# Decode keys in plain fp32, prepared two steps ahead, with part sums by matmul, in a hybrid encoder layer

## The chip, the cores and the metric

The kernel runs as one program on one core of a Trainium2 chip. Its time is the device time of one execution in microseconds. A profile of one execution is read beside it. The engines are PE (TensorE; PEld is its weight load), DVE (VectorE), ACT (ScalarE), POOL (GpSimd) and SP (SyncE, which here only issues DMAs).

## What is computed

One layer of a streaming encoder, for a prompt of 1024 tokens and for 8 decode sequences of 16 new tokens each, 9 tiles of 128 tokens in all; the model width is 1024. Cut to what matters:

```
def trunk_layer(x, p, ...):
    h = rmsnorm(x, g_mix)
    q_a, k_a, v_a, q_b, k_b, v_b = split_heads(h, w_in)     # 2 groups of 8 heads x 64
    # group A, all the past:  z = q k / 8
    #   w = exp(log_sigmoid(z) + reverse cumulative sum of log_sigmoid(-z));  a = w v
    # group B, own chunk of 64 and the 8 before it:
    #   o_b = softmax(q k / 8 + rel_table[clipped distance]) v
    # decode: the keys and values of the past come from caches
    #   (A: 1024 rows, B: 512 rows a sequence), then the 16 new ones
    mix = concat(rmsnorm per head(a), rmsnorm per head(o_b))
    x = x + mix @ w_out
    h = rmsnorm(x, g_ffn)
    x = x + (silu(h @ w_gate) * (h @ w_up)) @ w_down        # d_ff 2816
    x = x + sigmoid(rmsnorm(x, g_ple) @ w_ple_gate) * (p @ w_ple_proj)
    return rmsnorm(x, g_final), new keys and values
```

## The kernel before, in words

**Precision.** Most products are made of fp32 numbers split in two float32r parts, a high one and a low one (the remainder). `mm3` (L104 to L107) multiplies them as three matmuls: high by high, high by low, low by high. A split is a cast on ACT and a subtraction (`sub`, L109) on DVE or POOL; `Chunks` (L124 on) does it for weights and cache rows: `raw` issues the DMA (L134), `pair` gives the two tiles, `parts` casts on ACT (L149) and subtracts on POOL.

**Order.** The program is written with Python generators. `project`, `dec`, `att` and the smaller ones yield after each step, and `advance(main, side, ratio)` interleaves two of them. The framework then plans each engine's queue in simulated time, with program order as priority; a later instruction can go ahead of an earlier one that waits, if its tiles have room. On the chip each engine's queue runs in that planned order. Tiles come from pools of SBUF or PSUM banks; a new pool may lie where a closed one lay, and its tiles then wait for the old ones there.

**Stages.**
1. `x` is loaded, normed and transposed in nine tiles (`transposed`, L182; `normed`, L192).
2. `qkv` projects to queries, keys and values in twelve loads of 256 columns. `loads` begins with A's queries. A query step (`queries`) uses weights as the stationary operand and three token tiles (384 columns) as the moving one; a step of keys or values (`others`) uses one token tile. Keys are turned on PE (L255). High and low parts go to DRAM (`qkT`, `vhl`). 36 steps run alone, 30 more beside decode A (2.2 decode steps to one), the rest beside attention (1.95 attention steps to one).
3. `decode(grp, ...)`, for group A (4 chunks of 256 cache rows a sequence) and later B (2 chunks): a step of kind "k" turns 256 keys on PE (L385), casts them to high parts on ACT (L387) and subtracts low parts on DVE, then makes scores by `mm3` against a block-diagonal query (`scores`); a step of kind "v" splits values on ACT and POOL, flips the weights (`flip`) and accumulates (`outputs`, L457, L458). Each step's inputs are prepared one step ahead; `finish` picks the diagonal, sums parts with the constant `sel` (L474), norms, and writes to DRAM.
4. `attention` treats the prompt in 8 pairs of heads, A's four and then B's four, each with 2 heads of 8 query tiles: units. Per unit: `scores` (L564, L565, then sigmoids and a scan for A, a reduction with bias and an exp for B); five units later `flip` (L598, cast L602, subtraction); one later `outputs` (L621, L622). The product gives two halves on 128 partitions (from the high and the low parts of v); ACT copies one half (L628) and DVE adds (L629). After a pair, `finish` turns it (L640), norms it (L642 to L660) and writes it to DRAM (`mixp`, L663).
5. Beside attention B run decode B, then `embed` (the projection of p, L782 to L794), then `half_out`: `mix` reads `mixp` and `mixs` back, turns it (L829) and splits it; then the upper half of the output projection is added to `x1` in SBUF (L849).
6. After attention: mix of pairs 4 to 7, the lower half of the output projection with norm and transposes (`lower`), the feed-forward, the gated embedding, the final norm.

**PSUM, eight banks.** Up to the end of decode A: left t=2, o=2, s=1 (the stack `first`), right d=2, a=1 (`dstack`). For attention: left s=2, t=3, and right o=3 for the rest of the projection, opened after both earlier stacks close. Then right d=2, a=1 for decode B, and m=2 for the mix.

Of the kernel before, what the change touches and what calls it, by code (L numbers as in the profile page):

```python
# [22 lines left out]
P = 128  # L23
# [11 lines left out]
VLAG = (2, 1)  # L35
# [3 lines left out]
def tile_hymba_step(  # L39
# [55 lines left out]
    V.memset(zero, 0.0)  # L95

# [107 lines left out]
    mixp = [dram.tile([NP * P, P], F32, name=f"mixp{i}") for i in range(8)]  # L204
    proj = dram.tile([NT * P, D], F32, name="proj")
    mixs = [dram.tile([8 * P, HD], F32, name=f"mixs{i}") for i in range(2)]
# [5 lines left out]
    def qkv(ch, hT, stg):  # L212

        def parts(n, src, scale=1.0):
            hl = [stg.tile([P, 384], F32R, name=f"st{x}", tag=f"st{x}", bufs=1 + (x == "h"))[:, :n] for x in "hl"]
# [12 lines left out]
        def queries(grp, c, wts):  # L228
            wh, wl = wts
            for pr in range(2):  # L230
                m = slice(pr * P, (pr + 1) * P)
                for g in range(3):
# [3 lines left out]
                    transposed_out(grp, 0, c * 2 + pr, g, parts(384, ps_, HD**-0.5))  # L236
                    yield

        def others(grp, w, c, wts, gs):

            wh, wl = wts
            for g in gs:
# [14 lines left out]
                else:  # L257
                    for o in range(3):
                        sv = stg.tile([P, 4, 2, HD], F32R, name="sv", tag="sv", bufs=2)
# [21 lines left out]
        loads = [(0, 0, 0), (0, 0, 1), (0, 1, 0), (0, 1, 1), (0, 2, 0), (0, 2, 1),  # L281
# [26 lines left out]
    def decode(grp, ch, dk):  # L308
# [12 lines left out]
        new = {}  # L321
        for what in "qk":
            for x in range(2):
                t_ = dk.tile([P, 4, P], F32R, name=f"s{what}{x}")
                nc.sync.dma_start(t_.bitcast(F32), qkT[grp]["qk".index(what)][x][:, :, NP * P :].rearrange("c p n -> p c n"))
                new.setdefault(what, []).append(t_)
# [3 lines left out]
        new["v"] = [sv[:, :, :, x, :] for x in range(2)]  # L330
        qbd = []
        for i in range(2):
            pair = [dk.tile([P, 4, P], F32R, name=f"qbd{i}{j}") for j in range(2)]
            for t_ in pair:
                G.tensor_copy(t_, zero.unsqueeze(1).broadcast_to([P, 4, P]))
            qbd.append(pair)
        yield
# [14 lines left out]
        def prepare(i):  # L352
# [10 lines left out]
            if c == 0:  # L363
                q = st["q"] = qbd[n % 2]
                for part in range(2):
                    for half in range(2):
                        s = slice(half * 64, half * 64 + 64)

                        flat = q[part].rearrange("p a b -> p (a b)")[s]
                        dst = bass.AP(  # L370
                            tensor=flat.tensor,
                            offset=flat[:, half * 16 : half * 16 + 1].offset,
                            ap=[flat.ap[0], [160, 4], [1, 16]],
                        )
                        G.tensor_copy(dst, new["q"][part][s, :, b * 16 : b * 16 + 16].bitcast(F32))
# [4 lines left out]
            nk = 272 if last else 256  # L380
            kh, kl = ch.pair(4, nk)
            for m in range(2):
                pt = ps["d"].tile([P, 512], F32, name="pt", tag="T")
                for pr in range(4):
                    T.transpose(pt[:, pr * P : (pr + 1) * P], raw[:, m, pr * P : (pr + 1) * P], ident)  # L385
                pv = pt.rearrange("p (k n) -> p k n", k=4)
                A.copy(kh[:, :, m * P : (m + 1) * P], pv)  # L387
                sub(V, kl[:, :, m * P : (m + 1) * P], pv, kh[:, :, m * P : (m + 1) * P])
            if last:
                for dst, src in zip((kh, kl), new["k"]):  # L390
                    G.tensor_copy(dst[:, :, 256:272], src[:, :, b * 16 : b * 16 + 16].bitcast(F32))
            split[i] = kh, kl, None
# [13 lines left out]
        def scores(st, c, kh, kl):  # L406
# [5 lines left out]
            for pr in range(4):  # L412
                mm3(sc, q[0][:, pr], q[1][:, pr], kh[:, pr], kl[:, pr], pr == 0, pr == 3 and (grp == 1 or not last))
# [5 lines left out]
            else:  # L419
                mx = dk.tile([P, 1], F32, name="mx", tag="mx", bufs=4)  # L420
                V.tensor_tensor_reduce(w, sc, bias[:, own], 1.0,
                                       -3e38 if st["mx"] is None else st["mx"], ALU.add, ALU.max, accum_out=mx)
                st["mx"] = mx

        def weights(st):
# [8 lines left out]
            else:  # L434
# [3 lines left out]
                V.tensor_scalar(mx, mx, -1.0, None, op0=ALU.mult)  # L438
                A.activation(w, w, AF.Exp, bias=mx, accum_out=sm)
# [8 lines left out]
        def outputs(st, c, vh, vl, wt):  # L448
# [11 lines left out]
            if c == 0:  # L460
                add(wt[:, 0], *new["v"], True, False)
# [3 lines left out]
        def finish(st):  # L465
            b, acc = st["b"], st["acc"]
            own = dk.tile([P, 2, 64], F32, name="own", tag="own", bufs=2)
            av = acc.rearrange("p q (h d) -> p q h d", h=4)
            for h in range(4):
                s = slice(h * 32, h * 32 + 32)  # L470
                (V.tensor_copy if h % 2 else A.copy)(own[s], av[s, :, h, :])
            po = ps["d"].tile([P, 64], F32, name="po", tag="T")
# [12 lines left out]
            nc.sync.dma_start(mixs[grp][b * P : (b + 1) * P, :], ow)  # L485

        for i in range(RAWS - 1):
            fetch(i)
        prepare(0)
        for i, (kind, n, c) in enumerate(seq):  # L490
            if i + RAWS - 1 < len(seq):
                fetch(i + RAWS - 1)
            if i + 1 < len(seq):
                prepare(i + 1)
            h, l, wt = split.pop(i)
            if kind == "k":
                scores(batch[n], c, h, l)
                if c == nkc - 1:
                    weights(batch[n])
            else:  # L500
                outputs(batch[n], c, h, l, wt)
                if c == nkc - 1:
                    finish(batch[n])
            yield


    def attention(qp, ap_, ps, lag):
        def prepare(p8):
            grp, pr = divmod(p8, 4)
            st = {"pr": pr, "grp": grp}  # L510
            if grp:
                st["rs"] = ap_.tile([P, NP, 2], F32, name="rsum", tag="rsum", bufs=2)
            return st

        def head(st, hh):
# [4 lines left out]
            hd = {}  # L520
            qk = ap_.tile([P, 2 * D], F32R, name="qk", tag="qk", bufs=2)
            vk = ap_.tile([P, 2 * D], F32R, name="vk", tag="vk", bufs=2)
            for dst, parts in ((qk[:, :D], (qh, ql)), (qk[:, D:], (kh, kh)), (vk[:, D:], (kl, kl))):
                for i in range(2):
                    nc.sync.dma_start(dst[i * 64 : i * 64 + 64].bitcast(F32), parts[i][hs, :D])
            hd["qq"], hd["kkh"], hd["kkl"] = qk[:, :D], qk[:, D:], vk[:, D:]
            vv = vk[:, :D].rearrange("p (t x d) -> p t x d", t=NP, x=2)
            hc = ((pr % 2) * 2 + hh) * P
            nc.sync.dma_start(
                vk[:, :D].bitcast(F32).rearrange("p (t n) -> p t n", t=NP),  # L530
                vhl[grp][pr // 2, : NP * P, hc : hc + P].rearrange("(t p) n -> p t n", p=P),
            )
            hd["v"] = vv
            st[hh] = hd
# [3 lines left out]

        def bias(st, hh):
            toep = ap_.tile([P, (8 - hh * 2) * P], F32, name="toep", tag=f"keep{1 + hh}")[:, :640]  # L540
            nc.sync.dma_start(toep, rel[st["pr"] * 2 + hh])
            G.memset(toep[0:64, 576:640], NEG)
            G.memset(toep[64:128, 0:64], NEG)
            st[hh]["toep"] = toep

        def scores(st, hh, t):
# [11 lines left out]
            for lo, hi in ((0, cut), (cut, n)):  # L558
# [12 lines left out]
                else:  # L571
                    m = ap_.tile([P, 1], F32, name="mxp", tag="mxp", bufs=6)
                    V.tensor_tensor_reduce(w[:, lo:hi], sc, hd["toep"][:, 640 - n + lo : 640 - n + hi], 1.0,
                                           -3e38 if mx is None else mx, ALU.add, ALU.max, accum_out=m)
# [5 lines left out]
            else:  # L580
                V.tensor_scalar(mx, mx, -1.0, None, op0=ALU.mult)
                A.activation(w, w, AF.Exp, bias=mx, accum_out=st["rs"][:, t, hh : hh + 1])
# [23 lines left out]
        def outputs(st, hh, g, wt):  # L606
# [4 lines left out]
            po = ps["t"].tile([P, 512], F32, name="pt", tag="T")  # L611
            order = [2 * g] + [kb for kb in range(base, 2 * g + 2) if kb != 2 * g]
            for i, kb in enumerate(order):
# [8 lines left out]
                T.matmul(dst, lhsT=vs, rhs=wtl[:, kb - base, c0:c1], start=False, stop=(i == nkb - 1))  # L622

            if hh == 0 and g == 0:
                st["ob"] = ap_.tile([P, D], F32, name="ob", tag="ob", bufs=1)
# [419 lines left out]
```

## Time and profile before

| | us |
|---|---|
| median of 3 runs | 1995.54 |
| lowest, highest | 1991.24, 1997.32 |
| profiled execution, its own time | 1995.02 |
| its span, first to last instruction | 1993.2 |
| PE busy in the span | 1859.9 |
| mean granted TensorE clock | 0.971 |

Line numbers (L105) are those of the kernel before. An engine's busy time is the union of its records; PE's records overlap, since a matmul starts before the one ahead of it has ended. So a PE that is shown busy may still have room, and the distance between two starts says more. In a list of stages each row has the window, its length, and for each engine the busy time and the number of records; then the granted clock, the busy share of the DMA engines and their GB/s. In a list of groups the last two parts are busy time with the mean of one in ns, and the idle time just before, with what ended it. In a list of waits the figures are total time, times, longest.

### The profile page before, as it was taken

To read this page: it belongs to the slowest core of one execution; us is meant where nothing else is said; L and a number is where in the kernel's file an instruction comes from. 1 tells how busy PE (TensorE), PEld (TensorE's weight loads), DVE (VectorE), ACT (ScalarE), POOL (GpSimd) and SP (SyncE) were. 2 spreads that over 40 slices of the span, in tenths; PEclk is the share of its full clock that TensorE was granted. 3 is DMA by queue.
4 is the path that set the end of the run, shared out by engine and by line. 5 is a ranking of instruction groups with operands and counts; after the bars stand their busy time and mean duration, and the time that the engine had idled before them with its cause. 6 is when DMAs were issued, how large, how long until landed. Compare 5 with 4: busy or idle time off the path is not lost.

```text
span 1993.2 us, 29599 instructions
## 1 busy us (share of the span) xinstructions
PE 1859.9 (93%) x11682; PEld 1737.9 (87%) x11682; DVE 828.1 (42%) x1573; ACT 740.4 (37%) x1595; POOL 716.5 (36%) x602
## 2 busy tenths in 40 slices
PE   5999999789997888879699999999999999999998
PEld 4999998679996777668589999999999999999898
DVE  5112445537767566464352213213213213213635
ACT  5214555547666667563333111111111111111442
POOL 4113744547645454022123232232232232232355
PEclk8999999899998899989799999999999999999999
DMA  5546766545547486592211111111111111111133
GB/s 188 184 167 195 225 221 206 171 129 140 160 131 220 135 205 161 168 267 60 85 49 64 43 43 43 43 43 43 43 43 43 43 43 43 43 43 43 33 96 127
DMA packets 164682, 220.70 MB, mean 111 GB/s; under 512 B 14912, under 2 KB 116160, under 8 KB 164544
## 3 DMA queue, kind: packets, MB, share of 16 engines
q1 hardware_dynamic: 164544, 218.82, 36.5%
q8 instruction: 92, 1.51, 0.3%
q14 instruction: 46, 0.38, 0.1%
HBM read 168.97 MB, written 49.81 MB: 110 GB/s over the span
## 4 chain that ended last, share of the span: by engine, by line
PE 53%; DMA 4%; issue 3%; ACT 1%; POOL 1%; DVE 1%; SPq 0%; POOLq 0%; ACTq 0%
PE ps L105 16%; PE ps L106 15%; PE ps L107 15%; DMA proj<-pjo 1%; PE acc L105 1%; PE acc L106 1%; PE acc L107 1%; DMA mixn<-mixp 1%; PE pt L188 1%; DMA qk<-qT1l 1%; DMA vk<-kT1l 0%; PE pt L598 0%; POOL dlo L110 0%; PE pt L829 0%; DMA vk<-v 0%
## 5 line engine op out<-in xcount | busy, mean ns | idle before, releaser
L110 POOL TENSOR_TENSOR wlo<-wraw,whi 128x1024 fp32r<-128x1024 f32 (+1 forms) x112 | 263.1, 2369 | 606.6 <-ACT whi L149 597.1
L105 PE MATMUL ps<-hUh,whi 128*128 128x384 f32 x1056 | 352.9, 334 | 2.2 <-DVE sg L912 2.2
L106 PE MATMUL ps<-hUl,whi 128*128 128x384 f32 x1056 | 353.0, 334 | 0.0
L107 PE MATMUL ps<-hUh,wlo 128*128 128x384 f32 x1056 | 352.9, 334 | 0.0
L149 ACT CAST whi<-wraw 128x1024 fp32r<-128x1024 f32 (+1 forms) x112 | 108.5, 1018 | 319.7 <-PE ps L107 227.4
L928 DVE TENSOR_TENSOR x<-x,ps 128x512 f32<-128x512 f32 x198 | 136.0, 687 | 158.1 <-PE ps L107 158.1
L105 PEld LDWEIGHTS ps<-hUh,whi 128*128 128x128 f32 x1056 | 198.2, 188 | 3.0 <-DVE sg L912 2.6
L106 PEld LDWEIGHTS ps<-hUl,whi 128*128 128x128 f32 x1056 | 198.2, 188 | 0.4
L107 PEld LDWEIGHTS ps<-hUh,wlo 128*128 128x128 f32 x1056 | 198.2, 188 | 0.0
L107 PE MATMUL ps<-whi,hTl 128*128 128x256 f32 x576 | 165.7, 288 | 0.0
L105 PE MATMUL ps<-whi,hTh 128*128 128x256 f32 x576 | 165.4, 287 | 0.1
L106 PE MATMUL ps<-wlo,hTh 128*128 128x256 f32 x576 | 164.7, 286 | 0.0
L106 PE MATMUL ps<-wlo,acth 128*128 128x512 f32 x396 | 156.2, 394 | 0.0
L105 PE MATMUL ps<-whi,acth 128*128 128x512 f32 x396 | 155.3, 392 | 0.0
L107 PE MATMUL ps<-whi,actl 128*128 128x512 f32 x396 | 153.8, 388 | 0.0
L110 POOL TENSOR_TENSOR dlo<-draw,dhi 128x1024 fp32r<-128x1024 f32 x48 | 117.2, 2445 | 101.6 <-ACT dhi L149 99.1
L914 DVE TENSOR_TENSOR tmp<-sg,ps 128x384 f32<-128x384 f32 x66 | 36.6, 554 | 235.4 <-PE ps L107 235.4
L912 DVE TENSOR_TENSOR sg<-tmp,ps 128x384 f32<-128x384 f32 x66 | 36.5, 554 | 196.5 <-ACT tmp L911 196.4
L110 POOL TENSOR_TENSOR actl<-tmp,acth 128x384 fp32r<-128x384 f32 x66 | 66.6, 1010 | 133.7 <-ACT acth L915 133.7
L578 DVE TENSOR_TENSOR_SCAN keep<-keep,zero 128x128 f32<-128x128 f32 (+4 forms) x64 | 97.5, 1528 | 37.1 <-ACT keep L570 36.6
L105 PEld LDWEIGHTS ps<-whi,hTh 128*128 128x128 f32 x576 | 109.7, 190 | 0.5 <-DVE stl L221 0.3
L106 PEld LDWEIGHTS ps<-wlo,hTh 128*128 128x128 f32 x576 | 109.7, 190 | 0.2
(188 smaller groups left out, 4400.4 us busy)
## 6 DMA issues: line engine op xcount, KB each, us to landing
draw<-in_cache_sb_k SPq DMA_DIRECT2D x32, 512.0 KB, 4.7
draw<-in_cache_sb_v SPq DMA_DIRECT2D x32, 512.0 KB, 3.9
wraw<-in_w_in SPq DMA_DIRECT2D x12, 1024.0 KB, 6.2
wraw<-in_w_gate SPq DMA_DIRECT2D x11, 1024.0 KB, 5.4
wraw<-in_w_up SPq DMA_DIRECT2D x11, 1024.0 KB, 5.4
wraw<-in_w_down SPq DMA_DIRECT2D x11, 1024.0 KB, 5.0
v<-sv SPq DMA_DIRECT2D x36, 256.0 KB, 2.4
x<-in_x_prompt SPq DMA_DIRECT2D x16, 512.0 KB, 6.8
```

What stands on the lines that cost most here:

```text
L105: T.matmul(out, lhsT=ah, rhs=bh, start=start, stop=False)
L106: T.matmul(out, lhsT=ah, rhs=bl, start=False, stop=False)
L107: T.matmul(out, lhsT=al, rhs=bh, start=False, stop=stop)
L110: eng.tensor_tensor(out, a, hi.bitcast(F32), op=ALU.subtract)
L149: A.copy(h[:, o], v[:, o])
L188: T.transpose(pt[:, j * P : (j + 1) * P], h[:, c : c + P], ident)
L578: V.tensor_tensor_scan(rev, rev, zero[:, 0:1].to_broadcast([P, n]), 1.0, op0=ALU.mult, op1=ALU.add)
L912: V.tensor_tensor(out[0][:, f, s], t_, ps, op=ALU.mult)
L914: V.tensor_tensor(t_, sg[:, f, s], ps, op=ALU.mult)
L928: V.tensor_tensor(x1[t][:, o], x1[t][:, o], ps, op=ALU.add)
```

## The change

What it does, part by part:
- **Keys of decode** stay in fp32 after their turn: one tile `kT` (3 buffers) in place of a high and a low one, half copied by ACT, half by DVE; the query is the sum of its two parts; one fp32 matmul replaces `mm3`. Key turns use bank pool t in place of d. Inputs are prepared `AHEAD` = 2 steps ahead, the diagonal is copied at once and the rest of `finish` comes two steps later. B's cache rows have 3 buffers in place of 4.
- **Banks.** o=2 is opened once, on the right, for the whole projection; attention has t=4 in place of 3; decode B has d=1.
- **Order of loads.** A's keys come before its queries.
- **Sign.** B's queries, bias and rel tables are negated, and the softmax takes a minimum and `scale=-1`, so that the maximum needs no negation (L435, L581).
- **Part sums.** `outputs` of attention only copies both halves (ACT, 128x256); `turn`, per head, sums and turns them with a fp32 matmul against `halves` (two stacked identities). `outputs` comes two units after `flip`.
- **Heads.** `values` loads v apart from `head`; both are issued at the unit t=1 instead of 3, B's first head at t=6 of pair 3.
- **Embedding** runs along decode B (one step to 0.55), its tiles turned one ahead, `pjo` with 2 buffers.
- **Mix.** `mix` fetches two pieces ahead, and takes pairs as they finish; pair 7 is taken from SBUF; `mixs` is written in its final layout.
- **Residual.** The upper half's sum goes to DRAM (`resid`) and is read to `x1` after attention's SBUF is free.

The core of the diff:

```diff
-VLAG = (2, 1)
+VLAG, AHEAD = (2, 1), 2
...
+    halves = cst.tile([P, HD], F32, name="halves")
+    V.tensor_tensor(halves, ident[:, :HD], ident[:, HD:], op=ALU.add)
...
-        loads = [(0, 0, 0), (0, 0, 1), (0, 1, 0), (0, 1, 1), (0, 2, 0), (0, 2, 1),
+        loads = [(0, 1, 0), (0, 1, 1), (0, 0, 0), (0, 0, 1), (0, 2, 0), (0, 2, 1),
...
-            kh, kl = ch.pair(4, nk)
+            kT = dk.tile([P, 4, 272], F32, name="kT", tag="kT", bufs=AHEAD + 1)
             for m in range(2):
-                pt = ps["d"].tile([P, 512], F32, name="pt", tag="T")
+                pt = ps["t"].tile([P, 512], F32, name="pt", tag="T")
...
-                A.copy(kh[:, :, m * P : (m + 1) * P], pv)
-                sub(V, kl[:, :, m * P : (m + 1) * P], pv, kh[:, :, m * P : (m + 1) * P])
+                (A.copy, V.tensor_copy)[m](kT[:, :, m * P : (m + 1) * P], pt.rearrange("p (k n) -> p k n", k=4))
...
-                mm3(sc, q[0][:, pr], q[1][:, pr], kh[:, pr], kl[:, pr], pr == 0, pr == 3 and (grp == 1 or not last))
+                T.matmul(sc, lhsT=q[:, pr], rhs=kT[:, pr, :nk], start=(pr == 0),
+                         stop=(pr == 3 and (grp == 1 or not last)))
...
-            if i + 1 < len(seq):
-                prepare(i + 1)
+            if i + AHEAD < len(seq):
+                prepare(i + AHEAD)
...
-            own, other = slice(hh * 64, hh * 64 + 64), slice(64 - hh * 64, 128 - hh * 64)
-            tmp = ap_.tile([P, 256], F32, name="obt", tag="obt", bufs=1)
-            A.copy(tmp[own], po[other, :256])
-            V.tensor_tensor(st["ob"][own, g * 256 : g * 256 + 256], po[own, :256], tmp[own], op=ALU.add)
+            A.copy(st["ob"][:, g * 256 : g * 256 + 256], po[:, :256])
+
+        def turn(st, hh):
...
+            pt = ps["t"].tile([P, 512], F32, name="pt", tag="T")
+            for t in range(NP):
+                T.matmul(pt[:, t * HD : (t + 1) * HD], lhsT=st["ob"][:, t * P : (t + 1) * P], rhs=halves,
+                         start=True, stop=True)
+            own = st["osb"][:, :, hh * HD : (hh + 1) * HD]
+            A.copy(own, pt.rearrange("p (t d) -> p t d", t=NP))
...
-    banks(first, "left", t=2, o=2, s=1)
+    banks(right, "right", o=2)
+    banks(first, "left", t=2, s=1)
...
-    banks(left, "left", s=2, t=3)
-    banks(right, "right", o=3)
+    banks(left, "left", s=2, t=4)
...
-    banks(dstack, "right", d=2, a=1)
+    banks(dstack, "right", d=1, a=1)
...
-    beside = chain(dec, embed())
-    advance(att, beside, 1.3, 42)
+    next(dec)
+    advance(att, dec, 0, 6)
+    beside = along(dec, embed(), 0.55)
+    advance(att, beside, 1.3, 40)
...
+        if k < 7:
+            nc.sync.dma_start(src, mixp[k][g * 384 : g * 384 + n * P, :].rearrange("(t p) c -> p t c", p=P))
+        else:
+            src = pairs[7]["osb"][:, g * 3 : g * 3 + n]
...
+                nc.sync.dma_start(resid[t * P : (t + 1) * P, cs], xs)
...
-    side = half_out()
+    side = chain(half_out(), mix(range(4, 7)))
     advance(att, side, 1.0)
+    for _ in side:
+        pass
+    for _ in mix([7]):
+        pass
+    w_b = [out_weights(1, c) for c in range(2)]
     left.close()
...
+    for t in range(NT):
+        nc.sync.dma_start(x1[t], resid[t * P : (t + 1) * P, :])
```

More of the change, by code (lines that the diff above doesn't have):

```diff
@@ L329, in decode @@
                           vhl[grp][:, NP * P :, :].rearrange("c p n -> p c n"))
[L330 to L337, printed above, removed]
+        new_v = [sv[:, :, :, x, :] for x in range(2)]
+        qbd = [dk.tile([P, 4, P], F32, name=f"qbd{i}") for i in range(2)]
+        for t_ in qbd:
+            G.memset(t_, 0.0)
         batch = [{"b": b} for b in range(8)]
@@ L364, in prepare @@
                 q = st["q"] = qbd[n % 2]
[L365 to L375, printed above, removed]
+                for half in range(2):
+                    s = slice(half * 64, half * 64 + 64)
+                    flat = q.rearrange("p a b -> p (a b)")[s]
+                    dst = bass.AP(
+                        tensor=flat.tensor,
+                        offset=flat[:, half * 16 : half * 16 + 1].offset,
+                        ap=[flat.ap[0], [160, 4], [1, 16]],
+                    )
+                    G.tensor_copy(dst, new_q[s, :, b * 16 : b * 16 + 16])
                 st["w"] = dk.tile([P, nkc * 256 + 16], F32, name="wdec", tag="w", bufs=3)
@@ L502, in decode, with attention @@
                 if c == nkc - 1:
-                    finish(batch[n])
+                    diagonal(batch[n])
+                    late[i + AHEAD] = batch[n]
+            if i in late:
+                finish(late.pop(i))
             yield
-    def attention(qp, ap_, ps, lag):
+        for st in late.values():
+            finish(st)
+    def attention(ap_, ps, lag):
         def prepare(p8):
@@ L668, in run @@
             ws, wts = {}, {}
-            for i in range(len(units) + lag + 2 + 2):
+            for i in range(len(units) + lag + 4):
                 if i < len(units):
                     pr, hh, t = units[i]
-                    if t == 3:
+                    if t == 1:
+                        values(st[pr], hh)
                         if hh == 0:
@@ L776, in embed, with turned @@
         wj = ch.load(w_ple_proj[0].rearrange("(k p) c -> p k c", p=P), 2, D)
-        for t in range(NT):
+        def turned(t):
             pn = pp.tile([P, 256], F32, name="pn", tag="pn")
@@ L799, in chain, with along @@
             yield from p_
-    beside = chain(dec, embed())
-    advance(att, beside, 1.3, 42)
+    def along(a, b, ratio):
+        due = 0.0
+        for _ in a:
+            yield
+            due += ratio
+            while due >= 1.0:
+                due -= 1.0
+                if next(b, "end") != "end":
+                    yield
+        yield from b
+    next(dec)
+    advance(att, dec, 0, 6)
+    beside = along(dec, embed(), 0.55)
+    advance(att, beside, 1.3, 40)
     for _ in beside:
@@ new lines, in turn_mix, with mix @@
+    def turn_mix(k, g, srcs):
+        pt = ps["m"].tile([P, 384], F32, name="pt", tag="M")
+        for o, src in enumerate(srcs):
+            T.transpose(pt[:, o * P : (o + 1) * P], src, ident)
+        h, l = hT.rows(g, k)
+        gk = g_out[:, k : k + 1]
+        A.activation(h, pt, AF.Copy, scale=gk)
+        V.scalar_tensor_tensor(l, pt, gk, h.bitcast(F32), op0=ALU.mult, op1=ALU.subtract)
+    def mix(ks):
+        got = []
+        for k in ks:
+            while k not in done:
+                yield
+            for g in range(3):
+                got.append((k, g, fetch_mix(k, g)))
+                if len(got) > 2:
+                    turn_mix(*got.pop(0))
+                yield
+        for x in got:
+            turn_mix(*x)
@@ L834, in mix @@
             yield
     def half_out():
-        for k in range(4):
-            yield from mix(k)
+        yield from mix(range(4))
         for c in range(2):
```

227 lines of the change are left out of this document (111 added, 116 removed).

## The prediction

> **What bounds the kernel now.** I read the page first (busy shares, slices), then the busy time by stage, the same for the projection's tile alone, then single timelines, groups and waits where a term needed a price.
>
> ```profile
> span 1993.2 us, 29599 instructions
> PE 1859.9 (93%) x11682; PEld 1737.9 (87%) x11682; DVE 828.1 (42%) x1573; ACT 740.4 (37%) x1595; POOL 716.5 (36%) x602
> PE   5999999789997888879699999999999999999998
> PEclk8999999899998899989799999999999999999999
> ```
>
> The profiled execution took 1995.02 us around its span of 1993.2, so 1.8 us lie outside; the median of the runs is 1995.54. I make the sum against 1995. The last 23 slices are full: that is the feed-forward, which the change does not touch. The time to be had lies in the first slice and between slices 7 and 20. By stage:
>
> ```profile
> core 0: us, PE busy (x) PEld busy (x) DVE busy (x) ACT busy (x) POOL busy (x), PEclk, DMA share, GB/s
> 17.80:56.00 38.20, 28.55 (x142) 26.36 (x143) 19.21 (x26) 14.02 (x25) 13.75 (x16) 0.82 0.45 155
> 160.00:325.00 165.00, 165.00 (x1407) 164.68 (x1406) 70.69 (x104) 82.65 (x182) 78.36 (x81) 1.00 0.67 211
> 325.00:415.00 90.00, 65.47 (x428) 58.40 (x427) 44.22 (x65) 42.91 (x92) 51.07 (x38) 0.85 0.49 158
> 415.00:600.00 185.00, 182.65 (x1337) 172.67 (x1336) 123.98 (x162) 119.47 (x293) 107.38 (x82) 1.00 0.56 153
> 600.00:770.00 170.00, 137.73 (x965) 125.01 (x965) 115.55 (x297) 118.17 (x270) 89.81 (x113) 0.91 0.68 186
> 770.00:850.00 80.00, 67.04 (x400) 55.80 (x399) 42.52 (x140) 47.23 (x118) 12.39 (x15) 0.98 0.57 158
> 850.00:900.00 50.00, 38.96 (x236) 33.55 (x235) 33.10 (x118) 34.15 (x84) 10.44 (x10) 0.86 1.01 269
> 900.00:960.00 60.00, 59.76 (x318) 50.86 (x317) 28.93 (x80) 17.61 (x42) 9.93 (x6) 1.00 0.17 41
> 960.00:998.00 38.00, 20.39 (x107) 16.14 (x105) 12.15 (x26) 13.45 (x26) 9.88 (x6) 0.73 0.41 120
> ```
>
> These are: the start of the projection; decode A beside the projection; the end of decode A; attention on group A beside the projection's rest; attention beside decode B; beside the embedding; beside the mix transposes; beside the half output projection; the tail. What a PE matmul really occupies is the distance between two starts, which is shorter than its record:
>
> ```profile
> start us, us, engine line op out<-in xcount [idle before <-releaser]
> 229.06 0.28 PE L106 MATMUL ps<-wlo,hTh 128*128 128x256 f32 x1
> 229.18 0.28 PE L107 MATMUL ps<-whi,hTl 128*128 128x256 f32 x1
> 229.54 0.56 PE L474 MATMUL po<-own,sel 128*128 128x64 f32 x4
> 229.93 0.28 PE L397 MATMUL pt<-ident,wn 128*128 128x128 f32 x1
> ...
> 1200.17 0.33 PE L106 MATMUL ps<-hUl,whi 128*128 128x384 f32 x1
> 1200.34 0.34 PE L107 MATMUL ps<-hUh,wlo 128*128 128x384 f32 x1
> 1200.51 0.39 PE L105 MATMUL ps<-whi,acth 128*128 128x512 f32 x1
> 1200.74 0.39 PE L106 MATMUL ps<-wlo,acth 128*128 128x512 f32 x1
> ```
>
> A split matmul over 256 columns takes 0.12 us of PE, one over 384 takes 0.17, one over 512 takes 0.23. At 0.12 each, the 428 matmuls of 325 to 415 are 51 us of work: 39 us are empty, more than the busy column admits. From 600 to 770, 965 x 0.12 = 116, 54 empty. From 770 to 850, 108 of the 400 are the embedding's (18 outputs of 6 matmuls) at 0.23: 25 + 292 x 0.12 = 60, 20 empty. From 850 to 900, 236 x 0.12 = 28, 22 empty. From 960 to 998 some 13 to 16 of 38, 22 empty. So 325 to 998 holds about 157 empty us; 160 to 325 and 900 to 960 hold none. From 600 to 900 no engine is full (DVE 0.64, ACT 0.67): that stretch is bound by waits between engines.
>
> The hole at 325 has one reason:
>
> ```profile
> 160.00:325.00 165.00, 107.26 (x767) 96.90 (x766) 4.65 (x11) 7.96 (x21) 1.00 0.67 211
> 325.00:415.00 90.00, 3.70 (x28) 3.24 (x27) 0.00 (x0) 0.37 (x1) 0.85 0.49 158
> 415.00:600.00 185.00, 120.56 (x710) 103.08 (x709) 8.94 (x18) 10.88 (x24) 1.00 0.56 153
> ```
>
> That is the projection's tile ps alone. It stops at 325 and comes back at 415. In the code its next steps write three new PSUM banks that lie where decode A's banks d and a lay (dstack closes before they open), so they can't begin while decode A runs.
>
> **The change, part by part.**
>
> *Banks kept.* With two o banks on the right for the whole projection, the 39 empty us can take projection work from the stage behind; nothing in that work needs attention or decode A. Stage 415 to 600 then loses 39 us of its PE work, 183 - 39 = 144, and gets 10 from the part sums below: 154. But DVE had 124 busy there. Some 10 go with its additions (L629 below, three of eight pairs) and 3 with the moved projection (a third of ps's 8.94): 111. No stage above runs DVE over 0.68 of its time: 111 / 0.68 = 163 us, 22 less. I credit **-20**; the ends are 0 (attention keeps its pace without cover) and -31 (PE alone decides).
>
> *Scores in fp32.* 192 groups of three split matmuls (0.36 us) become one matmul that the hardware runs as two records: L474, two fp32 matmuls in the code, is x4. What a record costs at 256 columns no row shows. Four 64-column records fill 229.54 to 229.93, 0.10 each, their weight loads included; a 128-column f32 transpose takes 0.11 (the next fence: eight in 0.87). Lower end: a record streams like a split one, 2 x 0.12 = 0.24, a gain of 0.12 x 192 = 23 us. Upper end: it scales from the 64 columns, 2 x 0.40 = 0.80, 84 us dearer; the transpose, twice as wide in nearly the same time, speaks against that. I scale the transpose, the nearest row: 2 x 0.22 = 0.44, +0.08 x 192 = 15 us of PE. The Trainium skill says against this edit (FP8 and Floating Point Precision, TensorE Precision Notes) that true FP32 makes 4 passes through the array; an estimate by that page is 4 x 0.12 = 0.48 and +23 us, with which the sum would be 1950; the two-record rows fit it if a record holds two passes. Two thirds of the groups are decode A's, where PE will be full: **+10**; decode B's 5 fall into empty time.
>
> ```profile
> 1016.98 0.87 PE pt L188 x8
> L110 DVE TENSOR_TENSOR dlo<-pt,dhi 128x512 fp32r<-128x512 f32 x96 | 63.8, 684 | 45.5 <-ACT dhi L387 45.0
> L387 ACT CAST dhi<-pt 128x512 fp32r<-128x512 f32 x96 | 54.5, 594 | 28.9 <-PE pt L385 24.9 <-PE sdec L107 1.5 <-issue 1.4
> L629 DVE TENSOR_TENSOR ob<-pt,obt 64x256 f32<-64x256 f32 x64 | 26.7, 417 | 24.7 <-ACT obt L628 24.0
> L628 ACT COPY obt<-pt 64x256 f32<-64x256 f32 x64 | 23.5, 367 | 47.3 <-PE pt L622 45.8 <-PE S L565 0.5
> ```
>
> In exchange a key chunk needs two copies (one ACT, one DVE) instead of two ACT casts and two DVE subtractions: over 48 chunks ACT loses 48 x 0.59 = 29 us and DVE about 48 x 0.75 = 36. Neither engine is full, so this only shortens waits; with keys prepared two steps ahead, PE's wait for ACT dhi and DVE dlo goes. I count it in the stage terms alone.
>
> *Part sums by matmul.* L629 (26.7 us of DVE) goes; L628 becomes a copy of 128x256 on ACT at about the same price. Per pair, 8 transposes (0.87 us) become 2 x 8 fp32 matmuls, 32 records of 0.10 to 0.11: 3.4. Over 8 pairs +20 us of PE, 10 in the full stage (counted above), 10 in empty time. Each turn waits on PE for ACT's last copy, with the next unit's scores queued behind it; outputs now come two units after their flip, which covers that.
>
> *B's pairs.* Pair 7 is turned from SBUF. Today, after attention ends:
>
> ```profile
> 971.81 2.90 POOL r_o L116
> 975.09 2.06 POOL osb L660 x2
> 977.16 3.69 DMA mixp<-osb
> 981.35 6.41 DMA mixn<-mixp
> 987.90 1.51 PE pt L829 x6
> ```
>
> The 3.7 + 6.4 of the two DMAs go: **-10**. r_o, its POOL multiply and the transposes stay. The residual now goes to DRAM and back (18 writes of 256 KB, 9 reads of 512 KB on SP's queue, once the attention's SBUF is free). The lower half starts with four accumulators of 12 x 0.23 = 2.8 us before it needs x1, 11 us. I take **+2**; ends 0 and +25 (all nine reads in the open at the 186 GB/s of stage 600 to 770, 4.7 MB).
>
> *Stage 600 to 900.* The embedding moves beside decode B, one step in 0.55, with its transposes one tile earlier and two pjo buffers.
>
> ```profile
> ACT pjo L793 <- DMA proj<-pjo: 19.0, 10, 5.3
> PE pt L829 <- DMA mixn<-mixp: 17.9, 6, 8.2
> ```
>
> ACT's 19.0 us for pjo hold up the flips behind them on ACT; mix now fetches two pieces ahead, worth perhaps 5 of the 17.9. Sum **-24**. The ends: 0, and -59 if the stage's DVE (191 busy, less 12 for keys and 15 for additions, 164) runs at 0.68 of 241 us instead of 300. Bias and rel tables are negated on POOL, nine operations of some 1.3 us (osb's two of 128x512 take 2.06 above, these are 640 wide); POOL is at 90 of 170, so they are hidden. Should POOL be late, the first score reduction of a head waits for it on DVE, with the flips' subtractions queued behind, 1.3 us each.
>
> *Keys before queries.* A query step needs three token tiles, a key step one. From 17.8 to 56 the 142 matmuls, mostly 0.17 us (384 columns), make 24 us of 38.2, at a clock of 0.82. Tiles arrive one by one, so **-8**, ends 0 and -14.
>
> Sum: -8 (start) +10 (fp32, decode A) -20 (415 to 600) -24 (600 to 900) -10 (tail) +2 (residual) = -50; 1995 - 50 = **1945 us**.
>
> **The rivals.**
> *Given back* (slower). The hole is filled, but attention A, without its projection cover, is bound by its own chain through ACT, DVE and POOL and keeps 185 us; each turn then waits on PE for the copy and stands in that chain, so the 35 us of new PE work are all exposed: 1995 + 35 - 8 - 10 = 2012. For it: DVE never passes 0.68. Against it: decode's chain gets shorter, and PE has 157 empty us. It decides if stage 415 to 600 is not shorter after the change.
> *The hole stays.* The planner may not place the later steps there, as their staging buffers (one pair of sq for keys, queries and values) or weights come late. Then the -20 is lost and the full stage 415 to 600 takes 10 us of part sums: 1945 + 20 + 10 = 1975.
> *More.* The waits from 600 to 900 go down to the DVE limit (-59 instead of -24), 1910; with fp32 records as cheap as split ones (decode A 128 x 0.12 = 15 less in place of 10 more) 1885.
>
> **How the numbers follow.** Forecast's own case, 1920 to 1968: 0.50. More, below 1920: 0.18. The hole stays, 1968 to 1989: 0.12. Within 0.3% (about what a measurement of this kernel can tell from no change), 1989 to 2001: 0.06. Given back, above 2001: 0.14. So faster 0.80, same 0.06, slower 0.14. The range runs from 1905 (half of the More case) to 2000.
>
> **What would show it.** The ps tile busy from 325 to 415 and no slice of PE below 9 before 400; L385's keys without lo parts and two score records per group, 0.22 us apart; 16 turn records a head, 1.7 us on PE; no mixp DMA behind the last osb; the last r_o near 930 instead of 971.8. Wrong would be: 325 to 415 still without ps; a stage 415 to 600 as long as before; PE waiting for ob copies; or lower waiting for the residual's reads.

## The result and the profile after

The changed kernel takes 1910.82 us in the median (1908.38 to 1914.1), the one before 1995.72 beside it: the ratio is 0.9579, with a 95% interval of 0.9558 to 0.9600. That is 85 us less; 50 were forecast. The profiled execution has a span of 1912.3 us.

The page of the changed kernel, its span, PE's busy time, and PE and its granted clock in 40 slices:

```profile
span 1912.3 us, 29326 instructions
PE 1858.0 (97%) x11682; PEld 1742.9 (91%) x11682; DVE 763.2 (40%) x1390; ACT 707.8 (37%) x1543; POOL 721.3 (38%) x563
...
PE   7999999999997899999999999999999999999998
...
PEclk9999999999998899999999999999999999999999
```

PE is busy as long as before, in a span that is 81 us shorter. Slices 0, 7 and 8 and those from 14 on are fuller; one hole is left, at slices 12 and 13, where the clock drops too. By stage (columns as before; the cuts are now at the end of decode A, 380, the end of the projection, 574, the first half output product, 832, the last head's norm, 908):

```profile
core 0: us, PE busy (x) PEld busy (x) DVE busy (x) ACT busy (x) POOL busy (x), PEclk, DMA share, GB/s
17.80:56.00 38.20, 37.59 (x303) 37.26 (x302) 18.33 (x30) 18.74 (x36) 13.17 (x15) 1.00 0.57 188
150.00:380.00 230.00, 229.71 (x1743) 220.90 (x1742) 88.67 (x137) 112.47 (x248) 127.69 (x100) 1.00 0.63 205
380.00:574.00 194.00, 191.50 (x1413) 181.46 (x1412) 133.69 (x156) 130.76 (x319) 110.89 (x83) 0.99 0.58 160
574.00:650.00 76.00, 58.24 (x341) 50.99 (x340) 42.93 (x70) 41.95 (x95) 47.18 (x45) 0.82 0.70 199
650.00:832.00 182.00, 175.28 (x1230) 159.43 (x1228) 113.81 (x371) 134.15 (x343) 74.34 (x77) 0.99 0.75 208
832.00:908.00 76.00, 74.25 (x403) 62.85 (x402) 29.48 (x65) 23.04 (x50) 19.11 (x12) 1.00 0.49 151
908.00:960.00 52.00, 51.30 (x248) 41.86 (x248) 27.57 (x44) 16.97 (x32) 8.99 (x11) 1.00 0.39 143
```

The busy column hides small gaps, as the prediction said. So in both traces I priced every matmul by the distance between starts where PE is full (split: 256 columns 0.120 us, 272 0.127, 384 0.173, 512 0.229; a product with 128 columns 0.062; f32 transposes 0.109; an fp32 record of 64 columns 0.111, of 256 0.216, of 272 0.229; the bf16 masks 0.039) and took the sum from the stretch. What is left is called empty; it is worked out, with an error of a few us. The cuts are the same events in each kernel (in the kernel before at 413, 597, 892, 976 and 1045).

| us of PE | before | after |
|---|---|---|
| priced work, whole span | 1774 | 1809 |
| empty, 17.8 to 56 (start) | 16.7 | 2.8 |
| empty, 150 to the end of decode A | 38.9 | 0.2 |
| empty, from there to the projection's end | 10.1 | 11.0 |
| empty, from there to the half output projection | 99.1 | 50.5 |
| empty, from there to the last head's norm | 12.4 | 3.8 |
| empty, from there to the feed-forward | 13.0 | 1.7 |

The work grew by some 36 and the empty time fell by some 117 over the whole span (the feed-forward's rose by 3), which is the 81 of the spans.

What made the hole in decode A: the five longest of PE's waits from 150 to 413 in the kernel before (total, times, longest). All seven add up to 23 us; the rest of the 39 must lie in gaps that the records cover, since a record is longer than the distance between two starts.

```profile
PE acc L457 <- DVE wt L110: 5.3, 3, 3.7
PE po L474 <- DVE own L471: 4.8, 3, 1.9
PE pt L397 <- DVE dlo L110: 3.9, 3, 1.7
PE acc L458 <- POOL dlo L110: 3.6, 3, 1.3
PE sdec L105 <- ACT dhi L387: 3.5, 6, 0.7
```

All that are left in the same window of the changed kernel; only the 0.3 for wt lies before 380, the end of its decode A:

```profile
PE ps L108 <- ACT st L253: 2.1, 1, 2.1
PE acc L457 <- DVE wt L113: 0.3, 1, 0.3
PE S L580 <- DMA qk<-kT0l: 0.3, 1, 0.3
```

The waits were decode's own, on several engines at once: PE stood between a short step of decode and the next, with no projection step to put there. Was the hole filled with projection work, as the prediction has it? The projection's tile ps alone, in the kernel before, to the end of decode A and to the end of the projection,

```profile
150.00:413.00 263.00, 119.41 (x860) 108.33 (x859) 5.08 (x12) 9.09 (x24) 0.95 0.61 193
413.00:598.00 185.00, 122.02 (x720) 104.57 (x720) 8.42 (x17) 10.82 (x24) 1.00 0.55 151
```

and in the changed kernel:

```profile
150.00:380.00 230.00, 113.92 (x831) 104.04 (x830) 4.63 (x11) 8.59 (x23) 1.00 0.63 205
380.00:574.00 194.00, 110.73 (x632) 93.10 (x630) 8.07 (x16) 9.37 (x21) 0.99 0.58 160
```

In part. Behind decode A the kernel before still has 720 matmuls of the projection to do, the changed kernel 632. Priced, that is 101.7 us against 90.7: 11 us of projection work came forward through the kept banks. Decode A's own rows hold no more of it than before, because keys first has put 14 us ahead of 150. The other 28 of the 39 us were not filled, they are gone. The end of decode A moves by -14 (start) - 39 (hole) + 9 (fp32 scores) + 11 (projection work) = -33 us, from 413 to 380.

The new PE work, as groups of the changed kernel (scores, L413; turns, L648):

```profile
L413 PE MATMUL sdec<-kT,qbd 128*128 128x256 f32 x256 | 61.1, 380 | 0.1
L648 PE MATMUL pt<-halves,ob 128*128 128x64 f32 x256 | 33.4, 269 | 0.4 <-ACT ob L639 0.4
```

One step of decode in its timeline, eight transposes and then eight records of scores:

```profile
243.84 1.04 PE L388 MATMUL pt<-ident,draw 128*128 128x128 f32 x8
244.71 1.89 PE L413 MATMUL sdec<-kT,qbd 128*128 128x256 f32 x8
```

There are two records to each fp32 matmul. The eight of 244.71 end 1.89 us later, the last of them lasts 0.38, so seven distances make 1.51: 0.216 each, 0.43 for a group against 0.36 split. The last head's turn, from the chain that ended last:

```profile
894.26 1.73 PE pt L648 x16
```

Sixteen records in 1.73 us: 0.108 each, 0.111 in the median of the distances.

### The profile page after: what moved, and what is told of

Same layout as the page of the kernel before. It is cut to its first block, busy times and chain, and to the rows that moved or that the text cites. A ratio compares the mean times of both kernels' runs of the same rounds, so it can differ in the third digit from the quotient of the medians.

```text
span 1912.3 us, 29326 instructions
## 1 busy us (share of the span) xinstructions
PE 1858.0 (97%) x11682; PEld 1742.9 (91%) x11682; DVE 763.2 (40%) x1390; ACT 707.8 (37%) x1543; POOL 721.3 (38%) x563
## 3 DMA queue, kind: packets, MB, share of 16 engines
q8 instruction: 92, 1.51, 0.3%
## 4 chain that ended last, share of the span: by engine, by line
PE 90%; DMA 4%; ACT 2%; POOL 2%; DVE 1%; issue 1%; SPq 1%; POOLq 0%; ACTq 0%; DVEq 0%
PE ps L108 21%; PE ps L109 21%; PE ps L110 21%; PE sdec L413 4%; PE pt L612 2%; PE pt L388 2%; PE acc L108 2%; PE acc L109 2%; PE acc L110 2%; PE po L636 2%; PE po L635 1%; PE S L579 1%; PE acc L457 1%; PE acc L458 1%; PE S L580 1%; PE pt L648 1%
## 5 line engine op out<-in xcount | busy, mean ns | idle before, releaser
L593 DVE TENSOR_TENSOR_SCAN keep<-keep,zero 128x128 f32<-128x128 f32 (+4 forms) x64 | 106.9, 1676 | 46.4 <-ACT keep L585 40.4
```

Of the source, the lines that this page charges most:

```text
L593: V.tensor_tensor_scan(rev, rev, zero[:, 0:1].to_broadcast([P, n]), 1.0, op0=ALU.mult, op1=ALU.add)
```

## The experiments

My first theory was the prediction's: kept banks let the projection fill decode A's hole. The rivals were that the gain lies elsewhere, and that PE work shows in full anywhere, since PE now has only 5% of empty time. All times are medians; ratios are to the kernel before on the same chip. The runs were taken on several chips, where the kernel before had medians from 1995.7 to 1999.4. So a small difference between medians can be the chip's: the ratios decide (0.001 is 2 us), and the spans of the traces stand beside them.

**Kept banks alone**, on the kernel before:

```diff
-    banks(first, "left", t=2, o=2, s=1)
+    banks(right, "right", o=2)
+    banks(first, "left", t=2, s=1)
...
-    banks(right, "right", o=3)
```

> The kernel before with one change: the projection's two PSUM banks are opened once, on the right, and kept to its end (no third bank later). Theory: the stretch 325 to 415, which had 39 us of PE empty, fills with projection steps; but attention A then has less cover, and part of it comes back as a hole where the projection ends (the changed kernel has 33 us empty from 575 to 650). Time about 1975, 20 less than before. Rival 1: the hole is worth its full 39 us, 1957. Rival 2: the banks alone do nothing, since decode A's one-step preparation still holds PE up: 1995.

Measured: 1986.4 us, ratio 0.9967 (0.9946 to 0.9988). That is 7 us by the ratio and 9 by the medians, between the theory and the second rival. In its trace, all instructions of the two stretches:

```profile
325.00:440.00 115.00, 113.24 (x920) 112.39 (x920) 44.46 (x71) 57.34 (x125) 68.79 (x57) 1.00 0.57 180
440.00:584.00 144.00, 121.48 (x740) 105.59 (x739) 107.22 (x134) 91.90 (x223) 75.25 (x54) 0.92 0.53 136
```

The hole is filled: PE has 0.8 us empty up to the end of decode A. But decode A now ends at 440 in place of 413, since 65 us of projection work have moved into it and only 38 of them fit the hole. Attention A then has little cover (projection steps that PE can run while attention waits): 45 us are empty behind decode A, against 10. Thirty-five of the 38 us are given back. What attention waits for there, in the same trace:

```profile
POOL w L579 <- DVE keep L578: 61.2, 30, 12.0
DVE keep L578 <- ACT keep L570: 16.8, 12, 8.2
```

It is group A's own chain, sigmoids on ACT, a scan on DVE, a product on POOL; DVE is busy for 107.22 of the 144 us, 0.74, and its scan (L578) alone is 18% of the chain that ended last in this stretch. Filling a hole with work that was the cover of a later stage moves the hole.

**Queries first**, on the changed kernel:

```diff
-        loads = [(0, 1, 0), (0, 1, 1), (0, 0, 0), (0, 0, 1), (0, 2, 0), (0, 2, 1),
+        loads = [(0, 0, 0), (0, 0, 1), (0, 1, 0), (0, 1, 1), (0, 2, 0), (0, 2, 1),
```

> The changed kernel with the old order of loads, A's queries before its keys. Theory: from 17.8 to 56 the changed kernel has 2.8 us of PE empty, the old one 16.7; the difference shifts everything behind it, since PE is full to the end of the projection: 8 to 14 us slower than the changed kernel, 1919 to 1925. Rival: the start is given back later, where attention waits on other engines: no difference, 1911.

Measured: 1931.9 us, ratio 0.9676 (0.9658 to 0.9693). The order of loads is worth 21 us by the medians, 17.5 by the spans, more than the theory's 8 to 14. The stretch from 17.8 to 56 in this run:

```profile
17.80:56.00 38.20, 28.41 (x140) 26.22 (x141) 18.89 (x26) 14.16 (x26) 11.62 (x14) 0.82 0.46 156
```

It is nearly the row of the kernel before again, 140 matmuls instead of 303; 17.1 us are empty. In this stretch PE waits 9.6 us for the low parts of the transposed tiles (hTl), here as in the kernel before; with keys first that wait is gone. All later stages are shifted by it and give none back.

**Turn by transposes**, on the changed kernel (8 transposes a head in two banks, a copy and an addition for each bank):

```diff
-                T.matmul(pt[:, t * HD : (t + 1) * HD], lhsT=st["ob"][:, t * P : (t + 1) * P], rhs=halves,
-                         start=True, stop=True)
...
+                    T.transpose(pt[:, t * P : (t + 1) * P], st["ob"][:, o : o + P], ident)
...
+                A.copy(half, pv[:, :, 0])
+                V.tensor_tensor(half, half, pv[:, :, 1], op=ALU.add)
```

> The changed kernel with each head's part sum made by 8 transposes (0.109 us each) and one DVE addition from PSUM in place of 8 fp32 matmuls (16 records of 0.111): 0.9 us of PE less a head, 14.6 in all, two DVE additions a head more. Theory: group A's half lies beside the projection, where PE is full, and shows: 7 us faster, 1904; group B's lies beside waits and shows only in part. Rival 1: PE is the bound throughout: 15 us faster, 1896. Rival 2: the additions stand in DVE's queue ahead of the flips' subtractions: 1911 or more.

Measured: 1907.0 us, ratio 0.9559 (0.9544 to 0.9574). The interval overlaps the changed kernel's, so the 4 us are not shown. The trace has 14.4 us less PE work and 6.6 more empty, and the span is 7.6 shorter: in the direction of the theory.

**Keys in one pass**, on the changed kernel. It leaves the low parts of queries and keys out of decode's scores:

```diff
-        qbd = [dk.tile([P, 4, P], F32, name=f"qbd{i}") for i in range(2)]
+        qbd = [dk.tile([P, 4, P], F32R, name=f"qbd{i}") for i in range(2)]
...
-            kT = dk.tile([P, 4, 272], F32, name="kT", tag="kT", bufs=AHEAD + 1)
+            kT = dk.tile([P, 4, 272], F32R, name="kT", tag="kT", bufs=AHEAD + 1)
```

> The changed kernel with decode's keys and queries as one float32r part: the low parts are left out of the scores, everything else is the same. A group of scores then takes one matmul of 0.12 us in place of two records of 0.216: 192 x 0.31 = 60 us of PE less, 40 of them in decode A. Theory: decode A ends up to 40 us earlier, but the projection's cover of attention shrinks by as much, and attention A alone can't go faster than its other engines: 20 to 30 us faster in the end, 1880 to 1890. Rival 1: PE is the bound everywhere, 60 us faster, 1851. Rival 2: the scores hide under other waits, 1911.

Measured: 1873.4 us, ratio 0.9382 (0.9364 to 0.9399): 37 us faster, between the theory and the first rival. The work falls by 61 us and the empty time rises by 22: 9 in decode A, 12 between the projection's end and the half output projection. About 0.6 us shows for each us of PE work. The theory's own reason does not show: attention A has the same length (195 us against 194) and 1 us more of empty time.

So kept banks alone do not make the gain, and I formed another theory: decode itself stopped waiting. Two runs take a part out of the changed kernel.

**One step ahead**, and **banks opened anew**:

```diff
-VLAG, AHEAD = (2, 1), 2
+VLAG, AHEAD = (2, 1), 1
```

```diff
-    banks(right, "right", o=2)
-    banks(first, "left", t=2, s=1)
+    banks(first, "left", t=2, o=2, s=1)
...
+    banks(right, "right", o=2)
```

> The changed kernel with decode's inputs prepared one step ahead in place of two (the key tile has two buffers, the rest of finish comes one step later). In the changed kernel decode A ends at 380, against 413 before, and the projection work that is left for attention is nearly the same (110.7 us of ps busy against 122.0), so its hole was not filled by moved work as in the banks experiment, it is not there. Theory: the second step ahead takes the waits out of decode A; without it decode A ends 20 to 30 us later, and the time is 1925 to 1940. Rival: the shorter chain of an unsplit key (one copy in place of a cast and a subtraction) does it, and one step is enough: 1911 to 1916.

> The changed kernel with the projection's two banks opened anew after decode A, as before, in place of kept. Theory: with decode A no longer waiting there is no hole for the projection to fill, and kept banks are worth little: 1911 to 1917. Rival (the forecast's term): they are worth 20 us, 1930, with PE empty at decode A's end again.

Measured: one step ahead 1919.3 us, ratio 0.9610 (0.9592 to 0.9627); banks opened anew 1914.4, 0.9582 (0.9561 to 0.9604). Both intervals overlap the changed kernel's, so in time neither is shown to be worth much. The 122.0 and 110.7 us of ps that the first expectation calls nearly the same differ by the 11 us of projection work that did move into decode A. In the traces PE is empty for 6.3 us in decode A with one step, and for about 10 with banks opened anew, against 0.2. The theory for the steps ahead (20 to 30 us) falls. The banks' theory holds for the time, but not for its reason: without kept banks there is a hole again, and 720 matmuls of the projection are left behind decode A, as in the kernel before. But from the projection's end to the half output projection 41 us are empty, against 50 in the changed kernel. What the kept banks fill, some 10 us, comes back there.

**New decode pieces in the kernel before.** The first has only keys and queries unsplit; the second has the whole new decode (two steps ahead, later finish, key turns in pool t), with the old banks and loads. Their edits to the kernel before are the decode lines of the diff; the first keeps `prepare(i + 1)` and pool d, and both keep the old sign and the old layout of `mixs`:

```diff
+            kT = dk.tile([P, 4, 272], F32, name="kT", tag="kT", bufs=2)
...
+                (A.copy, V.tensor_copy)[m](kT[:, :, m * P : (m + 1) * P], pt.rearrange("p (k n) -> p k n", k=4))
...
+                T.matmul(sc, lhsT=q[:, pr], rhs=kT[:, pr, :nk], start=(pr == 0),
```

> The kernel before with decode's keys and queries unsplit in fp32 and nothing else: still one step ahead, key turns in bank pool d, banks and loads as before. Two steps ahead alone (8 us) and kept banks alone (some 4 us) were each worth little in the changed kernel, so most of the 39 us that PE stood empty in decode A must go elsewhere. Theory: the key's shorter chain, a copy on ACT or DVE in place of a cast and then a subtraction, takes 20 us or more out of decode A's empty time, against 15 us more PE work: 1975 to 1990. Rival 1: the chain was not the wait, and the fp32 passes are exposed: 2005 to 2010. Rival 2: only all of it together does it: 1995.

> The kernel before with the whole new decode (unsplit keys, two steps ahead, finish later, key turns in bank pool t), banks opened anew and loads in the old order as before, attention and its part sums as before. Theory: the new decode empties the hole by itself: decode A has under 12 us of PE empty, as in the kernel with banks opened anew, and ends some 20 us earlier; 1965 to 1978. Rival: without kept banks the hole stays half, 1980 to 1990.

Measured: unsplit alone 1976.7 us, ratio 0.9888 (0.9858 to 0.9917); the whole decode 1976.7, 0.9889 (0.9858 to 0.9920). Both times lie in their theories' ranges; out of decode A the unsplit keys take 17 us, not the theory's 20 or more. Unsplit keys and queries gain 23 us although PE has 14 more to do. PE's waits of the first run from 150 to 413, all of them:

```profile
PE acc L452 <- DVE wt L110: 4.8, 3, 2.5
PE po L469 <- DVE own L466: 3.9, 3, 1.9
PE acc L453 <- POOL dlo L110: 2.4, 2, 1.3
PE sdec L407 <- DVE kT L383: 2.1, 1, 2.1
PE pt L382 <- ACT kT L383: 1.7, 2, 1.0
```

The waits behind a key's cast and subtraction (dhi, and the dlo before L397), 7.4 us, are gone, and 3.8 for the copies (kT) stand in their place; those of the weights and of the diagonal stay. Whether a key's shorter chain or the lighter queues of ACT and DVE do it, no run separates. The empty time in decode A goes in steps: 38.9 before, 22.4 with unsplit keys, 11.2 with the whole new decode, 0.2 with kept banks and keys first as well (1.5 in the run with queries first, so the last step is the banks'). From the projection's end to the half output projection it goes from 99.1 to 81.9 and 84.0. The second run, like the first, takes 1976.7: of what it saves in decode A (which ends at 395, in the first at 406) 4 us are left at the half output projection (865 against 869) and 1 at the end.

**Embedding after decode B**, and **embedding early**, on the changed kernel:

```diff
-    beside = along(dec, embed(), 0.55)
+    beside = chain(dec, embed())
```

```diff
-    advance(att, dec, 0, 6)
-    beside = along(dec, embed(), 0.55)
+    emb = embed()
+    advance(att, emb, 1.0, 6)
+    beside = along(dec, emb, 0.4)
```

> The changed kernel with the embedding after decode B, as before, in place of beside it (two buffers and the earlier transposes stay). Theory: the stretch from the projection's end to the half output projection, 99 us of PE empty before and 50 now, gets 15 to 25 us longer, since decode B and the embedding each leave PE waiting alone: 1926 to 1936. Rival: the second buffer for the embedding's output was what counted: 1911 to 1915.

> The changed kernel with six embedding steps beside the six attention steps that run alone while decode B's loads arrive (the changed kernel's largest hole, 33 us of PE empty from 575 to 650), the rest beside decode B at one step in 0.4. Theory: some 10 us of embedding work move into the hole: 5 to 10 us faster, 1901 to 1906. Rival 1: that stretch waits on POOL, ACT and DMA, and the embedding's cast and transposes lengthen their queues: 1911 to 1918. Rival 2: the work is missed later beside decode B: no difference.

Measured: after decode B 1924.4 us, ratio 0.9633 (0.9613 to 0.9654), slower than the changed kernel by 14 us by the medians, 11 by the ratios, 10 by the spans, less than the theory's 15 to 25; 7.3 us more are empty between the projection's end and the half output projection, and 1.6 more behind it. Early: 1916.5 us, 0.9593 (0.9570 to 0.9615), no gain. The work was meant for the hole at 574 to 650, and its longest wait there is for the embedding's own input, on PE's queue ahead of attention:

```profile
PE pt L802 <- DMA pn<-in_p_prompt: 11.6, 1, 11.6
```

**Pair 7 by DRAM**, on the changed kernel:

```diff
-            if grp * 4 + pr < 7:
+            if True:
                 nc.sync.dma_start(mixp[grp * 4 + pr][:, :].rearrange("(t p) c -> p t c", p=P), osb)
...
-        if k < 7:
+        if k < 8:
```

> The changed kernel with pair 7 written to DRAM and read back before it is turned, as the other pairs. Theory: the chain at attention's end gets a write and a read longer (3.7 + 6.4 us in the kernel before), with little left to hide it: 5 to 10 us slower, 1916 to 1921. Rival: the weights' split and the rest of the half output projection cover it: 1911.

Measured: 1919.6 us, ratio 0.9599 (0.9577 to 0.9621). That is 9 slower by the medians, 6 by the spans and 4 by the ratios; the intervals overlap, so in time it is not shown. The trace shows the mechanism, on the chain that ended last:

```profile
905.04 2.06 POOL osb L672 x2
907.12 6.98 DMA mixp<-osb
914.24 2.62 DMA mixn<-mixp
916.99 1.53 PE pt L870 x6
```

PE is empty for 9.4 us between the last norm and the feed-forward, against 1.7.

**Turn by transposes with the projection spread**, on the changed kernel, an attempt at a faster version: the edit of the transposes above, and

```diff
-    advance(project, att, 1.95)
+    advance(project, att, 2.4)
```

> The changed kernel with heads turned by transposes and a DVE addition, and the projection's rest spread over more attention steps (2.4 to one in place of 1.95), so that the projection's end comes later and the stretch of attention alone behind it is shorter. Theory: of the 33 us that PE is empty from 575 to 650 some 10 go: 1893 to 1900. Rival: decode B starts later and its waits move to the end, where less is left beside attention: 1907 to 1915.

Measured: 1931.4 us, ratio 0.9665 (0.9641 to 0.9689). The rival's reason, at a higher price than its 1907 to 1915: decode B ends at 813 in place of 786, attention's last head is done at 867, and 12 of the 18 outputs of the upper output projection are left alone behind it, where PE waits for its additions and for DMAs:

```profile
892.14 0.50 PE L108 MATMUL acc<-whi,hUh 128*128 128x512 f32 x1 [0.45 <-DVE xs L907]
900.17 0.80 PE L108 MATMUL acc<-whi,hUh 128*128 128x512 f32 x1 [4.97 <-DVE xs L907]
...
923.83 0.52 PE L874 MATMUL pt<-ident,mixn 128*128 128x128 f32 x3 [2.54 <-DMA mixn<-mixp]
```

No run points to a version that computes the same and is shown to beat the changed kernel.

## Why the prediction was right, and where it was not

The sign and the range were right, and so was the account of PE work. The point was 34 us too high: 1911 lies in the interval of More (below 1920, 0.18), not in the forecast's own (1920 to 1968, 0.50). By stage the forecast had +2 up to the end of decode A, -20 in attention A, -24 to the half output projection and -8 behind it. The traces have -33, +10, -37 and -25 (and +4 in the feed-forward). That the two figures up to the projection's end, -18 and -23, lie close is luck: they are made of different parts. By its steps:

- **fp32 scores.** Forecast 0.44 us a group and +15 us of PE; measured 0.43 and +14. Scaling from the transposes was the right choice among far ends, though no row had shown that an fp32 record costs per column what a transpose does. The estimate by the Trainium skill's four passes (FP8 and Floating Point Precision, TensorE Precision Notes), each priced at the 0.12 of a split record, was 0.48; the trace has two records of 0.216, 10% less.
- **Part sums.** Forecast +20, measured 16 x 16 x 0.111 - 64 x 0.109 = +21. A turn waits 0.4 us on PE for ACT's copies in the whole run: the two-unit lag covers it, as forecast.
- **Keys first.** Forecast -8 with an end at -14. The trace has 13.9 us less empty, and putting queries first costs 17.5 to 21. The reason held (PE's wait for hTl goes) and the size was off: behind the start PE is almost full to the projection's end (12 us empty in 518), so the better end was the value to take.
- **Banks kept.** This step failed. The prediction read the missing ps rows rightly: where the banks are opened anew, 720 matmuls of the projection are left behind decode A in the three runs that do so too. But it gave the hole "one reason", and it has two: nothing else could run there, and decode itself waited. The banks filled 11 of the 39 us. Filled by banks alone, 35 of 38 us come back in attention A; in the changed kernel some 10 come back behind the projection. The other 28 us went because decode stopped waiting: the whole new decode takes them out by itself (38.9 to 11.2). The sentence that fails is the one on keys, that the shorter chain "only shortens waits", counted "in the stage terms alone": in the kernel before, unsplit keys take 17 us out of the hole, and 17 more behind the projection.
- **Stage 415 to 600 at -20.** Attention A did not get shorter but 10 us longer (184 to 194); the projection's end comes earlier because decode A's does. DVE is at 133.69 of 194, 0.69, but its 0.68 is no limit: with banks alone it reached 0.74 in this stage.
- **Stage 600 to 900 at -24, with 15 us of new work hidden**, so 39 less empty; measured 49. The embedding beside decode B is worth 10 to 14 us by its run. The wait of ACT's pjo for its DMA, 19.0 us before, is not among the changed kernel's waits.
- **Tail at -10 and residual at +2.** Measured 20 us less empty from the half output projection on. The DRAM trip of pair 7 is 7.7 of them by the trace of its run (4 to 9 us in time, not shown). The residual's reads cost nothing that shows: 1.7 us are empty in the whole stretch. What took the rest (the earlier split of the last weights, or mix taking pairs as they finish) was not tested.
- **The rivals.** "Given back" came true for the banks alone, not for the change. "The hole stays" is refuted. "More" is what happened, at its price of 1910 within the measurement's spread, but that is luck: its stage from 600 to 900 gave 37 us, not 59, and start, decode A and tail gave the rest.
- **A reading.** The page's full slices are the last 20, not the last 23 (slices 17 and 19, from 0, are at 7 and 6); no term hangs on it.

What stays open: which part of the new decode closes the step from 22.4 to 11.2 (two steps ahead, the later finish, or the key turns in pool t), and to what the whole new decode loses later what it saves there. Taken singly, the runs put unsplit keys at 23 us, keys first at 17 to 21, the embedding at 10 to 14, two steps ahead at 5 to 8, pair 7 at 4 to 9 and kept banks at 1 to 4, together 60 to 79 of the 85; the last three are not shown in time, and such values need not add up. The signs, the earlier heads, attention's fourth bank, the residual and the order of mix were not run alone.

## What to carry to other kernels

A hole in the busiest engine has two cures, other work in it or a shorter chain behind it; borrowed work that was the cover of a later stage moves the hole, and a shorter chain can remove it, though here what the whole new decode removed beyond the unsplit keys came back later. So ask of each hole what the engine waits for inside it, not only why nothing else runs there. And an operation that costs the full engine 20% more can pay if it takes a step out of the chain that this engine waits on, while here a change of order at the very start, ahead of a full engine, was worth all of its time.

## What the runs showed of the hardware

An fp32 matmul shows as two records here. At 256 columns they come 0.216 us apart, at 272 0.229, where a split record comes every 0.120 and 0.127; at 64 columns they come every 0.111, no faster than an f32 transpose of 128 (0.109). So a part sum over 64 columns costs twice what a transpose of the same tile costs. And of PE work taken out of a kernel whose PE is 97% busy by the page, 61 us, only 37 to 39 came out of the time.
